# Attention in head pairs: a masked gate bias spread by DMA, K projected transposed, no output transposes

## The chip, the cores and the metric

One core of a Trainium2 chip runs the whole kernel in one launch. The metric is the device time in microseconds (us) of one execution; smaller is better. TensorE (PE) multiplies matrices into PSUM (8 banks of 128 partitions x 512 float32), VectorE (DVE) and ScalarE (ACT) work on PSUM and SBUF, GpSimd (POOL) on SBUF only, and SyncE (SP) issues most DMAs. A matmul keeps one operand stationary (its "weights", up to 128 x 128) and streams the other one past it.

## The reference

A decoder trunk of two layers on 256 tokens of width 1024, float32. Layer 0 mixes tokens with a recurrence (RG-LRU), layer 1 with forgetting attention; each layer has a SwiGLU FFN (hidden width 2816) before and after its mixer, and RMS norms around every part. What the change touches is K, V and the gate, which are computed between the layers, and the attention:

```python
def shared_kv(h, g, w_kv, w_f, b_f):
    hn = rms_norm(h, g)
    kv = (hn @ w_kv).reshape(Bn, S, 2, N_HEADS, HEAD_DIM)      # 16 heads of 64
    k, v = ...
    log_f = jax.nn.log_sigmoid((hn @ w_f + b_f).astype(jnp.float32))
    c = jnp.cumsum(log_f, axis=1).transpose(0, 2, 1)

def forgetting_attention(xq, w_q, w_o, k, v, c):
    q = (xq @ w_q).reshape(...) * (HEAD_DIM ** -0.5)
    for blk in range(S // Q_BLOCK):                            # 2 blocks of 128 queries
        logits = q_block @ k[:, :, :end].T + c[q] - c[k]       # per head
        logits = jnp.where(kpos[None, :] <= qpos[:, None], logits, -jnp.inf)
        p = jax.nn.softmax(logits, axis=-1)
        outs.append(p @ v[:, :, :end])
    return concat(outs) @ w_o
```

## The kernel before

The 256 tokens are two halves t = 0 and 1 of 128. Every weight matrix is read once, in units of 512 KB: `load_raw` issues the DMA on SP's queue into one of 5 raw buffers, and `split` cuts it into an upper part (ACT, L199) and the rest (DVE, L200), each float32r; 9 split units may wait. A product of activations and weights, both cut, takes three matmuls (`mm3`, L207 to L209), or, where the weights are stationary, one of 512 columns (upper and lower activations of both halves side by side) and one of 256 (`mmj`, L222 and L223).

PE's order is the program's order. It is written by hand: `run` and `run_ffn` go through the units with half 1 some units behind half 0, and the units with stationary weights (`tile_items`, `last_items`, through `still`) serve both halves at once on four PSUM banks that are "lent" to them. After each unit, and in the middle of a `still`, `tick` counts down the deferred functions (`defer`) and runs those that are due: transposes, statistics and parameters. The orders of ACT, DVE, POOL and SP are made by a scheduler, which goes by readiness in a model of its own and by the program's order; each engine then runs its queue in order. The memory pools of the FFN and of the attention share addresses: a tile of the next pool waits for the readers of the tile that it covers.

PSUM banks are given out by `bank`: 0 to 3 to accumulators ("mm"), 4 and 5 ("gt"), 6 and 7 ("tr"); `sparebank` takes a "tr" bank, or an "mm" one while 6 is lent.

K is projected like V, with the activations stationary, so that tokens lie on partitions. `heads_T` scales it, appends two columns to each head (a one and the negative gate sum `nck`), and transposes head by head: 8 transposes of 128 x 66 for each half and group of 8 heads. Q goes the same way (with the gate sum `cq` and a one), so that a matmul over 66 rows gives the logits with c[q] - c[k] in them.

The attention of half t goes in groups of four heads (t = 0, 128 keys) or two (t = 1, 256 keys): 4 and 8 groups. `logits` multiplies (L1128), adds the causal mask to the diagonal block (L1129), takes the maximum (L1131) and the exponentials with their sums (L1136). `turn` transposes the exponentials (L1144) and copies them (L1146). `values` multiplies by V with the exponentials stationary (L1155), 64 columns a head, and after 8 heads divides by the sums (L1158, L1160). `output` transposes that (L1168) and cuts it into `oh` and `ol` (L1171, L1172) for the output projection. Step i does logits(i), values(i-3), turn(i-2) and, where 8 heads are done, output. A string gives the order of units and steps ("0" and "1": a unit of half 0 or 1, first of w_q, then of w_o; "a0" and "a1": a step):

```python
    ATT_ORDER = ("0 0 0 0 0 0 0 0 a0 1 a0 1 1 1 a0 1 a0 1 a0 1 a0 a1 1 a0 "
                 "0 a1 a0 a1 0 a1 0 a1 0 a1 0 a1 0 a1 0 a1 0 a1 1 a1 1 a1 1 1 1 1 1 1")
```

Of the kernel before, what the change touches and what calls it, by code (L numbers as in the profile page):

```python
# [16 lines left out]
P = 128  # L17
# [27 lines left out]
def trunk_kernel(ctx: ExitStack, tc: tile.TileContext, A: dict, out: bass.AP):  # L45
# [21 lines left out]
    def bank(kind, hold=False):  # L67

        i = next(i for i in order[kind] if i not in held)
        assert i not in lent, (kind, i)  # L70
# [21 lines left out]
    def sparebank():  # L92
        return bank("mm" if 6 in lent else "tr")
# [125 lines left out]
    def mmj(b, wh, wl, k):  # L219

        tensor_work(3 * S)
        nc.tensor.matmul(pall[:, b, :], wh, xall[:, k, :, :].rearrange("p a b -> p (a b)"), start=k == 0, stop=False)  # L222
        nc.tensor.matmul(pall[:, b, :S], wl, xhi[:, k, :], start=False, stop=k == 7)  # L223
# [135 lines left out]
    state = {"p": 0, "a": 0, "b": 0}  # L359
# [143 lines left out]

    def ffn_items(pool_of, wg, wu, wd, post_g, next_dests, last=False, normed=False, lead=1):
# [4 lines left out]
        def hid_tiles():  # L509
            if not hid:  # L510
                for s in ("hhi", "hlo"):
                    hid[s] = pool_of().tile([P, 2, 22, P], F32R, tag=s, name=nm(s), bufs=1)
# [34 lines left out]
        def total(v, b, m):  # L547

            nc.scalar.activation(v, pall[:, b:b + m, S:], AF.Copy)
            nc.vector.tensor_tensor(v, pall[:, b:b + m, :S], v, ALU.add)  # L550

# [18 lines left out]
        def still(t, u, k0, b0):  # L570
            if k0 == 0:
                assert not set(held) & set(range(b0, b0 + 4)), held.keys()
                lent.update(range(b0, b0 + 4))
            for j in range(2):
                for b in range(4):
                    o = j * 512 + b * P
                    mmj(b0 + b, u.hi[:, o:o + P], u.lo[:, o:o + P], k0 + j)
                if j == 0:
                    tick()
            if k0 == 6:  # L580
                lent.difference_update(range(b0, b0 + 4))

        def tile_items(w, c0, b0, post):
            for k0 in range(0, 8, 2):
                def prep(k0=k0):
                    return split(load_raw(w[k0 * P:(k0 + 2) * P, c0:c0 + 512].rearrange("(k p) n -> p k n", p=P), P, 1024),
                                 P, 1024)

                def work(t, u, k0=k0):
                    still(t, u, k0, b0)  # L590
                    if k0 == 6:
                        post(b0, 4)
                items.append((prep, work))

        def last_items(c0):
            for k0 in range(0, 8, 2):
# [7 lines left out]
                def work(t, u, k0=k0):  # L604
                    still(t, u, k0, 4)
# [27 lines left out]
    def run_ffn(ends, lag_out=LAG):  # L633
# [6 lines left out]
        state["a"] = state["b"] = i2  # L640
        run(n, MID, lag_out)
# [13 lines left out]
    def other_gains():  # L655
# [4 lines left out]
        defer(5, lambda: gains_T(grow, 40, 16))  # L660
# [324 lines left out]
    def dests_l1(t, hid):  # L985
        zx[t] = [hid[s][:, t, :8, :] for s in ("hhi", "hlo")]
        return [(GI["kv"], *zx[t]), main_dest(GI[("ffn1", 1)], t)]
# [3 lines left out]
    def kv_tiles():  # L991
        lp = ctx.enter_context(tc.tile_pool(name="kv", bufs=1, reuse_waits="tile"))
        kv["kT"] = lp.tile([HA, NH, S], F32, name="kT")
        kv["v"] = [lp.tile([P, D], F32, name=f"v{t}") for t in range(2)]
        for n in ("nck", "cq", "lf"):
            kv[n] = [lp.tile([P, NH], F32, name=f"{n}{t}") for t in range(2)]
        kv["bfb"] = lp.tile([P, 2 * NH], F32, name="bfb")[:, :NH]
# [7 lines left out]
        cm = kv["cmask"] = lp.tile([P, P], F32, name="cmask")  # L1005
        nc.gpsimd.memset(cm, 0.0)
        nc.gpsimd.affine_select(out=cm, in_=cm, compare_op=ALU.is_ge, fill=NEG, base=0,
# [355 lines left out]
```

## Time and profile before

| | |
|---|---|
| median of 3 runs | 1009.94 us (1008.15 to 1010.61) |
| the profiled execution | 1007.29 us, its span 1005.6 us |
| granted TensorE clock | 0.999 of full speed |
| PE busy | 991.0 us of the span |
| DVE, ACT, POOL busy | 665.3, 566.1, 51.5 us |
| DMA | 178.90 MB, 178 GB/s on average |

The profile is of one execution. A line such as L1128 is a line of the kernel. PE rows are matmuls, PEld rows their weight loads; a float32 matmul that is not float32r shows as two records, a transpose as one. A matmul's own duration overlaps that of the next one, so its slot is read from the distance of the starts, or from the chain of waits, which is cut at the starts. A groups' row gives: line, engine, operation, output<-input, shapes, count | busy us, mean ns | idle before. A timeline's row gives: start, duration, engine, line and operation, and in brackets the idle time before.

### The profile page before, as it was taken

To read this page: it belongs to the slowest core of one execution; us is meant where nothing else is said; L and a number is where in the kernel's file an instruction comes from. 1 tells how busy PE (TensorE), PEld (TensorE's weight loads), DVE (VectorE), ACT (ScalarE), POOL (GpSimd) and SP (SyncE) were. 2 spreads that over 40 slices of the span, in tenths; PEclk is the share of its full clock that TensorE was granted. 3 is DMA by queue.
4 is the path that set the end of the run, shared out by engine and by line. 5 is a ranking of instruction groups with operands and counts; after the bars stand their busy time and mean duration, and the time that the engine had idled before them with its cause. 6 is when DMAs were issued, how large, how long until landed. Compare 5 with 4: busy or idle time off the path is not lost.

```text
span 1005.6 us, 13910 instructions
## 1 busy us (share of the span) xinstructions
PE 991.0 (99%) x5302; PEld 847.3 (84%) x5302; DVE 665.3 (66%) x768; ACT 566.1 (56%) x742; POOL 51.5 (5%) x113
## 2 busy tenths in 40 slices
PE   8999999999999999999999999999999999999997
PEld 5887888889988888888898888888888888888885
DVE  5877664568998676664695577674477477666642
ACT  5656543559987555543565555553468566555431
POOL 1500000000003000000000000000020020000000
PEclk9999999999999999999999999999999999999999
DMA  6877656565427666545476766655555057665431
GB/s 230 280 263 204 190 161 197 154 181 151 141 78 250 212 188 187 188 158 185 114 227 218 209 191 184 192 189 168 168 168 168 2 188 237 184 199 195 155 121 42
DMA packets 91864, 178.90 MB, mean 178 GB/s; under 512 B 11790, under 2 KB 31318, under 8 KB 91798
## 3 DMA queue, kind: packets, MB, share of 16 engines
q1 hardware_dynamic: 90550, 176.89, 56.8%
q10 hardware_dynamic: 608, 1.06, 0.3%
q8 instruction: 41, 0.67, 0.3%
q0 software_dynamic: 640, 0.07, 0.1%
q14 instruction: 25, 0.20, 0.1%
HBM read 176.95 MB, written 1.05 MB: 177 GB/s over the span
## 4 chain that ended last, share of the span: by engine, by line
PE 70%; issue 21%; ACT 4%; DVE 4%; POOL 1%; DMA 0%; DVEq 0%; POOLq 0%; ACTq 0%
PE pall L222 21%; PE pall L223 11%; PE pall L209 10%; PE pall L208 10%; PE pall L207 10%; PE pall L845 1%; DVE wlo L200 1%; PE pall L214 1%; PE pall L215 1%; PE pall L216 1%; PE pall L1128 1%; ACT junk L236 1%; PE pall L1155 1%; ACT whi L199 1%; PE pall L1026 1%
## 5 line engine op out<-in xcount | busy, mean ns | idle before, releaser
L200 DVE TENSOR_TENSOR wlo<-raw,whi 128x1024 fp32r<-128x1024 f32 (+4 forms) x329 | 394.6, 1206 | 242.3 <-ACT whi L199 241.8
L199 ACT ACTIVATE whi<-raw 128x1024 fp32r<-128x1024 f32 (+4 forms) x329 | 342.1, 1044 | 290.3 <-PE pall L209 125.6
L222 PE MATMUL pall<-xall,whi 128*128 128x512 f32 x1216 | 424.7, 395 | 0.0
L223 PE MATMUL pall<-xall,wlo 128*128 128x256 f32 x1216 | 338.4, 278 | 0.0
L222 PEld LDWEIGHTS pall<-xall,whi 128*128 128x128 f32 x1216 | 228.1, 188 | 53.3
L223 PEld LDWEIGHTS pall<-xall,wlo 128*128 128x128 f32 x1216 | 228.8, 188 | 0.2
L207 PE MATMUL pall<-whi,hhi 128*128 128x512 f32 (+2 forms) x432 | 166.0, 384 | 0.0
L209 PE MATMUL pall<-whi,hlo 128*128 128x512 f32 (+2 forms) x432 | 165.0, 382 | 0.0
L208 PE MATMUL pall<-wlo,hhi 128*128 128x512 f32 (+2 forms) x432 | 164.8, 382 | 0.0
L209 PEld LDWEIGHTS pall<-whi,hlo 128*128 128x128 f32 x432 | 81.1, 188 | 15.1
L208 PEld LDWEIGHTS pall<-wlo,hhi 128*128 128x128 f32 x432 | 81.2, 188 | 14.7
L207 PEld LDWEIGHTS pall<-whi,hhi 128*128 128x128 f32 x432 | 81.2, 188 | 14.6
L207 PE MATMUL pall<-whi,xall 128*128 128x512 f32 (+2 forms) x168 | 67.1, 400 | 0.1
L208 PE MATMUL pall<-wlo,xall 128*128 128x512 f32 (+2 forms) x168 | 64.9, 386 | 0.4 <-DVE wlo L1226 0.2
L209 PE MATMUL pall<-whi,xall 128*128 128x512 f32 (+2 forms) x168 | 64.9, 386 | 0.1
L229 POOL TENSOR_SCALAR nv<-ss 128x1 f32<-128x1 f32 x24 | 10.9, 453 | 749.8 <-ACT junk L236 749.6
L208 PEld LDWEIGHTS pall<-wlo,xall 128*128 128x128 f32 x168 | 31.7, 189 | 7.5 <-DVE wlo L200 1.2
L209 PEld LDWEIGHTS pall<-whi,xall 128*128 128x128 f32 x168 | 31.5, 188 | 7.1 <-DVE xall L259 1.1
L207 PEld LDWEIGHTS pall<-whi,xall 128*128 128x128 f32 x168 | 31.6, 188 | 5.7 <-ACT xall L254 0.5
L567 ACT ACTIVATE hhi<-prod 128x1024 fp32r<-128x1024 f32 (+1 forms) x21 | 20.6, 980 | 25.2 <-DVE prod L563 25.2
L300 DVE SCALAR_TENSOR_TENSOR t<-pall,rstd,gb 128x512 f32<-128x512 f32 x16 | 11.9, 748 | 26.7 <-ACT junk L236 26.7
L557 ACT ACTIVATE sil<-sil 128x1024 f32<-128x1024 f32 (+1 forms) x21 | 20.6, 982 | 15.1 <-DVE sil L556 15.0
(190 smaller groups left out, 974.2 us busy)
## 6 DMA issues: line engine op xcount, KB each, us to landing
raw<-in_ffn_w_down_dram SPq DMA_DIRECT2D x88, 512.0 KB
raw<-in_ffn_w_up_dram SPq DMA_DIRECT2D x80, 512.0 KB
raw<-in_ffn_w_gate_dram SPq DMA_DIRECT2D x79, 512.0 KB
raw<-in_rg_w_in_dram SPq DMA_DIRECT2D x20, 504.0 KB
raw<-in_rg_w_out_dram SPq DMA_DIRECT2D x10, 504.0 KB
raw<-in_ffn_w_gate_dram SPq DMA_DIRECT2D x18, 256.0 KB
raw<-in_ffn_w_up_dram SPq DMA_DIRECT2D x16, 256.0 KB
raw<-in_w_kv_dram SPq DMA_DIRECT2D x8, 512.0 KB
```

Source lines behind the costliest of these rows:

```text
L199: nc.scalar.activation(hi[:parts, c:c + m], rawv[:, c:c + m], AF.Copy)
L200: nc.vector.tensor_tensor(lo[:parts, c:c + m], rawv[:, c:c + m], hi[:parts, c:c + m].bitcast(F32), ALU.subtract)
L207: nc.tensor.matmul(ps, xh, wh, start=first, stop=False)
L208: nc.tensor.matmul(ps, xh, wl, start=False, stop=False)
L209: nc.tensor.matmul(ps, xl, wh, start=False, stop=last)
L214: nc.tensor.matmul(ps, wh, xh, start=first, stop=False)
L222: nc.tensor.matmul(pall[:, b, :], wh, xall[:, k, :, :].rearrange("p a b -> p (a b)"), start=k == 0, stop=False)
L223: nc.tensor.matmul(pall[:, b, :S], wl, xhi[:, k, :], start=False, stop=k == 7)
L229: nc.gpsimd.tensor_scalar(v, ss[:, 0:1], ss[:, 1:2] if n == 2 else 0.0, D * EPS * f * f, ALU.add, ALU.add)
L300: nc.vector.scalar_tensor_tensor(t1[n], pf[n], r_in, gb[:, n * 512:(n + 1) * 512], ALU.mult, ALU.mult)
L557: nc.scalar.activation(s, s, AF.Silu)
L567: nc.scalar.activation(hv, pv, AF.Copy)
```

## The change

- **K** is projected with its weights stationary (`tile_items` with the moving operand of the normed stream, `z_moving`), so that it comes out with head dimensions on partitions, two heads on 128. It is scaled by the row of factors `rcp` and not transposed. For this the two FFN tiles `hhi` and `hlo` become one.
- **Q** is transposed in pairs of heads, 4 transposes instead of 8 for each half and group of 8 heads, without extra columns.
- **The gate** is no longer in the matmul. The gate sums are turned (`rows`), written to DRAM as 16 x 256, read back onto all 128 partitions (`nb0` 128 keys, `nb1` 256 keys for each head; 1 and 2 MB) on SP's queue, masked by POOL, and added to the logits in one DVE addition per step. c[q] is left out, since it drops out of the softmax.
- **Logits** take the two heads of a pair from partitions 0-63 and 64-127, into two banks; the sums are divided out before `turn`.
- **Values** have V stationary (64 columns) and the transposed exponentials moving, and write the two heads of a pair to partitions 0-63 and 64-127 of the result, which thus comes out transposed; `output` is gone.
- A step is values(i-3), turn(i-2), logits(i), and the order string begins the steps one unit earlier.
- `defer` has a flag `calm`: such a function runs only outside the first and the last unit of a `still` block. It is set for `rg_params`, the gains, `running` and `rows`. `sparebank` takes an "mm" bank whenever one of 0 to 3 is neither held nor lent.

```diff
     def sparebank():
-        return bank("mm" if 6 in lent else "tr")
+        return bank("mm" if any(i not in held and i not in lent for i in range(4)) else "tr")
...
-    def defer(n, fn):
-        pend.append([n, fn])
+    def defer(n, fn, calm=False):
+        pend.append([n, fn, calm])
...
-            if p[0] < 0:
+            if p[0] < 0 and not (p[2] and state["edge"]):
...
-    def mmj(b, wh, wl, k):
+    def x_moving(k):
+        return xall[:, k, :, :], xhi[:, k, :]
+
+    def mmj(b, wh, wl, k, moving):
         tensor_work(3 * S)
-        nc.tensor.matmul(pall[:, b, :], wh, xall[:, k, :, :].rearrange("p a b -> p (a b)"), start=k == 0, stop=False)
-        nc.tensor.matmul(pall[:, b, :S], wl, xhi[:, k, :], start=False, stop=k == 7)
+        both, upper = moving(k)
...
+        nc.tensor.matmul(o, wh, both, start=k == 0, stop=False)
+        nc.tensor.matmul(oh, wl, upper, start=False, stop=k == 7)
...
+    def still(u, k0, b0, moving=x_moving):
...
+        state["edge"] = k0 in (0, 6)
...
-        defer(5, lambda: gains_T(grow, 40, 16))
+        defer(5, lambda: gains_T(grow, 40, 16), True)
...
+        kv["ckT"] = lp.tile([NH, S], F32, name="ckT")
+        kv["dram"] = ctx.enter_context(tc.tile_pool(name="scratch", bufs=1, space=bass.MemoryType.DRAM)).tile(
+            [NH, S], F32, name="ckd")
...
+    def heads_T(pool, ps, t, n, scale, dst):
+
+        tok = pool.tile([P, 512], F32, tag="htok", name=nm("htok"), bufs=2)
+        nc.vector.tensor_scalar(tok, ps, rs[t][:, 0:1], scale, ALU.mult, ALU.mult)
+
+        def turn():
+            tp = bank("mm")
             for j in range(4):
...
+                nc.tensor.transpose(tp[:, j * P:(j + 1) * P], tok[:, j * P:(j + 1) * P], ident)
+            nc.scalar.activation(dst[:, 4 * n:4 * n + 4, :].rearrange("p a b -> p (a b)"), tp, AF.Copy)
+        defer(2, turn)
 
     def post_k(n):
-        return lambda t, ps: heads_T(pools["f"], ps, t, n, 1.0, (None, kv["nck"][t]), kv["kT"][:, :, t * P:(t + 1) * P])
+        def f(b, m):
+            kk = pools["f"].tile([P, 16 * HA], F32, tag="prod", name=nm("kk"), bufs=1)[:, :1024]
+            v = kk.rearrange("p (a b) -> p a b", a=4)
+            total(v, b, m)
+            nc.vector.tensor_tensor(kv["kT"][:, 4 * n:4 * n + 4, :], v, rcp["v"].unsqueeze(1).to_broadcast([P, 4, S]), ALU.mult)
+        return f
...
+    def rows(t):
+        pc = sparebank()
+        nc.tensor.transpose(pc[:NH, :P], kv["nck"][t], ident)
+        nc.vector.tensor_copy(kv["ckT"][:, t * P:(t + 1) * P], pc[:NH, :P])
+        if t == 1:
+            nc.sync.dma_start(kv["dram"], kv["ckT"])
...
-        proj_items(A["w_kv"], n * 512, 512, z_x, post_k(n))
+        tile_items(A["w_kv"], n * 512, 4 - 4 * n, post_k(n), z_moving)
...
     def att_tiles():
         ap = pools["a"]
...
+        src = kv["dram"].rearrange("h k -> (h k)").partition_broadcast(P).rearrange("p (h k) -> p h k", h=NH)
...
+            nb = ap.tile([P, NH, (t + 1) * P], F32, name=f"nb{t}")
+            nc.sync.dma_start(nb, src[:, :, :(t + 1) * P])
+            v = nb[:, :, t * P:]
+            nc.gpsimd.affine_select(out=v, in_=v, compare_op=ALU.is_ge, fill=NEG, base=0,
+                                    pattern=[[0, NH], [-1, P]], channel_multiplier=1)
...
         def logits(hg):
...
+            c = 4 + (hg % 2) * 2
+            lg = pall[:, c:c + 2, :S]
+            for j in range(np_):
+                for b in range(2):
+                    p = hg * np_ + j
+                    nc.tensor.matmul(lg[:, b, j * w:(j + 1) * w], att["q"][t][b * HD:(b + 1) * HD, p, :],
+                                     kv["kT"][b * HD:(b + 1) * HD, p, :w], start=True, stop=True)
...
+            nc.vector.tensor_tensor(v, v, bias, ALU.add)
...
+            nc.vector.reciprocal(sm, sm)
+            nc.vector.tensor_tensor(pe, pe, sm.unsqueeze(2).to_broadcast([P, per, w]), ALU.mult)
 
         def turn(hg):
-            tp = trbank()
+            tp = bank("mm", again=True)
...
         def values(hg):
...
+                        nc.tensor.matmul(po[b * HD:(b + 1) * HD, o:o + P], kv["v"][k][:, hd * HD:(hd + 1) * HD],
+                                         pT[:, (b * np_ + j) * nk + k, :], start=k == 0, stop=k == nk - 1)
+            if (p0 + np_) % 4 == 0:
...
+                nc.scalar.activation(oh_v, po, AF.Copy)
+                nc.vector.tensor_tensor(ol_v, po, oh_v.bitcast(F32), ALU.subtract)
...
-    ATT_ORDER = ("0 0 0 0 0 0 0 0 a0 1 a0 1 1 1 a0 1 a0 1 a0 1 a0 a1 1 a0 "
-                 "0 a1 a0 a1 0 a1 0 a1 0 a1 0 a1 0 a1 0 a1 0 a1 1 a1 1 a1 1 1 1 1 1 1")
+    ATT_ORDER = ("0 0 0 0 0 0 0 a0 0 a0 1 1 1 a0 1 1 a0 1 1 a0 1 a1 0 a0 0 a1 0 a0 0 a1 0 a1 0 a1 0 a1 0 a1 1 a1 1 a1 1 a1 1 a1 1 1 1 1")
...
-    defer(40, rg_params)
+    defer(40, rg_params, True)
...
-    run(n_kv)
+    run_ffn((n_v, n_kv, n_kv))
```

More of the change, by code (lines that the diff above doesn't have):

```diff
@@ L65, in trunk_kernel, with bank @@
     held = {}
-    def bank(kind, hold=False):
-        i = next(i for i in order[kind] if i not in held)
-        assert i not in lent, (kind, i)
+    def bank(kind, hold=False, again=False):
+        free = [i for i in order[kind] if i not in held and i not in lent]
+        i = free[-1 if again else 0]
         order[kind].remove(i)
@@ L604, in work @@
                 def work(t, u, k0=k0):
[L605 removed]
+                    still(u, k0, 4)
                     if k0 == 6:
```

182 lines of the change are left out of this document (82 added, 100 removed).

## The prediction, made before the changed kernel was run

> **What bounds the kernel now.** I read the page first: the busy times (part 1) and the shares of the chain (part 4).
>
> ```profile
> PE 991.0 (99%) x5302; PEld 847.3 (84%) x5302; DVE 665.3 (66%) x768; ACT 566.1 (56%) x742; POOL 51.5 (5%) x113
> PE 70%; issue 21%; ACT 4%; DVE 4%; POOL 1%; DMA 0%; DVEq 0%; POOLq 0%; ACTq 0%
> ```
>
> TensorE (PE) is never free; VectorE (DVE) and ScalarE (ACT) have a third and more of the span to spare. So the time is the length of PE's instruction stream plus its few waits, and what counts is how much stream an edit takes away, and whether a new wait opens. Next I asked for PE's waits: ten lines, from 2.1 us down to 0.2, about 7 us in all. The largest stands below them in PE's timeline:
>
> ```profile
> PE pall L699 <- issue: 2.1, 1, 2.1
> PE pall L208 <- DVE wlo L200: 0.2, 1, 0.2
> ```
>
> ```profile
> 82.58 0.28 PE L223 MATMUL pall<-xall,wlo 128*128 128x256 f32 x1
> 85.00 0.27 PE L699 MATMUL pall<-ident,prow 88*126 88x88 f32 x1 [2.13 <-issue]
> 85.05 0.48 PE L222 MATMUL pall<-xall,whi 128*128 128x512 f32 x1
> ```
>
> Last I read the chain of waits from 730 to 810 us, where the attention lies. It runs almost only over PE there, so its durations are slots in PE's stream: the transposes of Q and K (L1026), of the exponentials (L1144) and of the output (L1168), the logits (L1128) and the values (L1155). One block of each (a group of four heads has eight records, of two heads with 256 keys four):
>
> ```profile
> 745.20 0.44 PE pall L1026 x4
> 749.30 0.89 PE pall L1128 x8
> 778.77 0.87 PE pall L1128 x4
> 779.64 0.84 PE pall L1155 x8
> 780.48 0.45 PE pall L1144 x4
> ```
>
> **The change, term by term.** *Transposes.* The groups by line give their numbers:
>
> ```profile
> L1026 PE MATMUL pall<-ident,htok 128*66 128x128 f32 x64 | 9.6, 272 | 0.0
> L1168 PE MATMUL pall<-ident,ot 128*128 128x128 f32 x16 | 2.5, 280 | 0.1
> ```
>
> 64 head transposes are 16 blocks of four: 8 for K, 8 for Q. K's all go (it is now projected transposed), Q's are halved (a pair of heads fills 128 rows), and the 4 output blocks go (values now writes its result transposed). 16 blocks x 0.44 = **-7.0 us**; nothing covers PE, so all of it counts.
>
> *The wait at L699.* `rg_params` is deferred by 40 ticks and lands where its bank is still being emptied. `calm` puts it off to the middle of a unit. I take the 2.13 us idle as gone, **-2.1**; what is late next is a weight unit, and at 85 us the following matmul comes 0.05 us behind, so those weights are there.
>
> *K projection.* 96 matmuls of 512 columns become 64 pairs of 512 and 256: 49,152 columns either way. Rows of both kinds in PE's timeline:
>
> ```profile
> 539.43 0.40 PE L207 MATMUL pall<-whi,hhi 128*128 128x512 f32 x1
> 542.85 0.39 PE L207 MATMUL pall<-whi,hhi 128*128 128x512 f32 x1
> 560.11 0.39 PE L222 MATMUL pall<-xall,whi 128*128 128x512 f32 x1
> 563.58 0.39 PE L222 MATMUL pall<-xall,whi 128*128 128x512 f32 x1
> ```
>
> 15 matmuls in 3.42 us are 0.228 each, 10 pairs in 3.47 us 0.347 each: 96 x 0.228 = 21.9 against 64 x 0.347 = 22.2, **+0.3**. The moving operand is now read in pieces of 128 columns, which no row shows; a separate 256-column matmul costs half of a 512-column one (0.347 less 0.23 is 0.12), so shorter pieces have no visible price, and I take none. K's evacuation, one ACT copy and two DVE operations per half, lies beside the next 32 pairs, 11 us on the other four banks.
>
> *The gate's rows.* Two small transposes come in (`rows`). The nearest row is a small transpose between full matmuls, where a pair's L223 rows are otherwise 0.347 apart:
>
> ```profile
> 46.15 0.28 PE L223 MATMUL pall<-xall,wlo 128*128 128x256 f32 x1
> 46.36 0.25 PE L157 MATMUL pall<-ident,grow 40*128 40x40 f32 x1
> 46.54 0.49 PE L222 MATMUL pall<-xall,whi 128*128 128x512 f32 x1
> 46.87 0.28 PE L223 MATMUL pall<-xall,wlo 128*128 128x256 f32 x1
> ```
>
> 0.72 - 0.347 = 0.37 us for this one, against 0.11 for one of a block of four: 0.2 to 0.8 for two, I take **+0.5**.
>
> *Logits and values in half arrays.* Record counts stay, as the float32 matmul still takes two records. Today they cost 4 x 0.89 + 8 x 0.87 + 12 x 0.84 = 20.6 us. Now two heads sit in the two row halves (logits) or column halves (values). No row shows two matmuls in two halves. One bound: they run one after the other as today, 0. Other bound: the second record of one head overlaps the first of the other, so a block of eight takes five slots and one of four takes three. That saves 3 x 0.11 in each of 4 logit and 12 value blocks and 0.22 in each of 8 logit blocks: 1.3 + 4.0 + 1.7 = -7.0. Against it stands entering and leaving such a block: L157, with 40 rows, is the only row of a part of the array in a full stream, and it costs 0.37 - 0.11 = 0.26 more than a full-size transpose. 24 blocks x 0.26 = +6.2; the lower end is 0. So -7.0 to +6.2; I take the middle, **0**, since both rows and bounds are of equal size.
>
> The Trainium skill (TensorEngine Tiling (Array Packing), Key Properties) says that changing the tiling mode drains TensorE, which speaks against this edit; the L157 row agrees with it, and by that rule alone the sum would be 6.2 higher. The same page (Theoretical Speedup) gives up to 2x for a dimension of 64; as an estimate from it, 20.6 us would fall to 10.3, and no trace here shows it.
>
> *Waits in the softmax.* A step is now values, turn, logits, instead of logits, values, turn. Its chain today:
>
> ```profile
> 786.14 1.03 PE L1128 MATMUL pall<-kT,qT 66*128 66x256 f32 x4
> 787.21 0.43 DVE L1129 TENSOR_TENSOR pall<-pall,cmask 128x256 f32<-128x256 f32 x1 [2.39 <-PE pall L1128]
> 789.84 0.21 ACT L1136 ACTIVATION_READ_ACCUMULATOR pe<-pall,mx 128x1 f32 x1
> 794.94 0.61 PE L1144 MATMUL pall<-ident,pe 128*128 128x128 f32 x4
> 791.59 0.69 DVE L1160 TENSOR_TENSOR ot<-pall,sm 128x512 f32<-128x512 f32 x1 [0.41 <-PE pall L1155]
> 797.18 0.20 DVE L1158 RECIPROCAL sm<-sm 128x8 f32<-128x8 f32 x1 [1.72 <-ACT pe L1136]
> 797.03 0.60 ACT L1171 ACTIVATE oh<-pall 128x512 fp32r<-128x512 f32 x1
> ```
>
> From the logits' start at 786.14 to the exponentials' end at 790.05 it takes 3.9 us, and their transpose comes at 794.94: 4.9 us to spare. The new chain adds 0.26 (the addition covers 512 columns), a reciprocal (0.20) and a product (0.69, like L1160) ahead of the transpose: 5.1 with nothing in between, some 5.4 with two hand-overs. The new gap from logits to their transpose is their own 0.87, a unit (six matmuls of 0.228, 1.37), values 0.84, turn 0.45, logits 0.87, a unit, and values 0.84: 6.6 us. So about 1 us is spare. What can stand in between is a weight split:
>
> ```profile
> L200 DVE TENSOR_TENSOR wlo<-raw,whi 128x1024 fp32r<-128x1024 f32 (+4 forms) x329 | 394.6, 1206 | 242.3 <-ACT whi L199 241.8
> L199 ACT ACTIVATE whi<-raw 128x1024 fp32r<-128x1024 f32 (+4 forms) x329 | 342.1, 1044 | 290.3 <-PE pall L209 125.6
> ```
>
> One of them, 1.21 or 1.04 us, eats what is spare. Where two steps meet without a unit, and at the last output unit, which follows values(7) at once and needs the copy `oh` (0.60) and a subtraction like L1160 (0.69), PE waits 1 to 1.5 us each time. I take **+3.0** in all, from 0 to 8.
>
> *The bias.* 1 MB and 2 MB are broadcast from DRAM through SP's queue, and GpSimd masks each; DVE adds. What SP, GpSimd, ACT's table load and the DMA engines take today:
>
> ```profile
> 735.75 0.39 PE L209 MATMUL pall<-whi,hlo 128*128 128x512 f32 x1
> 731.38 6.13 SPq L187 DMA_DIRECT2D raw<-in_attn_w_o_dram  x4
> 738.51 0.33 SPq L352 DMA_DIRECT2D gb<-in_mix_post_g_dram  x1
> 741.02 18.88 SPq L187 DMA_DIRECT2D raw<-in_attn_w_o_dram  x4
> 317.05 0.29 POOL L1007 TENSOR_SCALAR_AFFINE_SELECT cmask<-cmask 128x128 f32<-128x128 f32 x1
> 752.69 1.28 ACT L1136 ACT_TABLE_LOAD   x1
> 750.00:800.00 50.00, 49.62 (x313) 43.12 (x312) 29.17 (x45) 33.84 (x95) 0.24 (x2) 1.00 0.28 85
> GB/s 230 280 263 204 190 161 197 154 181 151 141 78 250 212 188 187 188 158 185 114 227 218 209 191 184 192 189 168 168 168 168 2 188 237 184 199 195 155 121 42
> ```
>
> The first copy must wait for the FFN's tiles in the same memory, last read at 736 us (the first row). SP has a hole at 738 to 741. At some 200 GB/s, which weight loads reach in many of the 40 slices of the last row, 1 MB takes 5 us: landed by 744. The mask covers 16 times L1007's columns, at most 16 x 0.29 = 4.6 us: ready by 749. The first logits come at 736 + 7 units + transposes, about 747, and PE first waits for their result at the third step, four units and two steps later, about 755; the chain (5.4, and 1.28 for a table load) fits within a microsecond. The second copy has until about 767. DMA is at 28% there, so the loads behind it have room. Cost **0**, if the order on SP's queue is that. DVE gets about 8 us more work (12 products less 4, and the longer additions) in a stretch where it is busy 29 of 50 us: covered, but for the chain above.
>
> **Sum.** -7.0 - 2.1 + 0.3 + 0.5 + 0 + 3.0 + 0 = -5.3 us. The profiled execution took 1007.29 us with a span of 1005.6, and would take 1002.0 with 1000.3. Its time lies 2.65 below the median of the runs, so the median goes from 1009.94 to **1004.6**.
>
> **Rivals.** *Half arrays pair without a price*: -7.0 instead of 0, so 997.6. For it: PE has no other work between; against it: L157's 0.26. Chance 0.17. The Trainium skill's factor of two, cited above, stands on this side.
>
> *The softmax sets the step.* If one or two splits lie in each chain, 5.4 + 2 x 1.21 = 7.8 against 6.6, PE waits 1.2 us at most of the 12 turns, and with the ends some 8 to 11 us instead of 3: 1009.6 to 1012.6. Against it: in the second half's later steps no splits run. Chance 0.18. Half arrays at L157's price without pairing (+6.2), with 3 of waits, end at the same place, 1010.8; I count them here.
>
> *The bias comes late.* If SP holds the first copy behind the four loads that stand at 741.02 and wait until 759.9 for buffers, it lands near 765 and is masked by 769. PE reaches the first transpose at 755 and needs the bias some 6 us before that, so it waits about 769 + 6.7 - 755 = 21 us: 1001.6 + 21 = 1022.6 with the other waits covered by this one. It decides from 748 us on: each microsecond later than that is one of PE's. For it: SP's queue is in order and its loads wait long; against: the hole at 738. Chance 0.12: slower.
>
> *The calm tasks and the bank choice change nothing* (the L699 wait only moves): 2.1 less gain, 1006.7. Chance 0.05, and the forecast keeps 0.48.
>
> **Numbers.** About 0.3% (3 us) is what a measurement of this kernel can tell from no change: below 1006.9 is faster, above 1013.0 slower. The forecast's own range is 999 to 1010. Faster: most of the forecast (0.42), all of the first rival (0.17), the last one (0.04) and a bit of the second (0.03): 0.66. Slower: the bias (0.12), a tail of the second (0.04) and of the forecast (0.02): 0.18. The rest is 0.16. The range, 995 to 1013, takes in both bounds of the half arrays and the second rival, and leaves out the late bias.
>
> **What the profile after would show.** Right: no transposes of K or of the output, 16 of Q; L699's successor without the 2 us; blocks of logits and values whose slots differ from 0.89, 0.87 and 0.84 by little either way; a few PE waits on ACT or DVE between 736 and 806, 3 us in all. Wrong: value blocks of 0.5 us (half arrays pair), PE waits at most turns (softmax), a PE wait of over 5 us at the first turn with a DMA behind it (bias), or K pairs well over 0.347.

## The result

The changed kernel takes **1005.41 us** (median of 8 runs, 1004.71 to 1007.71) against 1008.22 for the kernel before in the same comparison: ratio 0.9968 (95% interval 0.9956 to 0.9980), **2.8 us faster**, where 5.3 were forecast. A second comparison gave 1005.72 against 1007.91, ratio 0.9973 (0.9962 to 0.9984). The profiled execution took 1004.95 us with a span of 1003.2, 2.34 and 2.4 less than before. The page after answers the two lines read first:

```profile
PE 985.8 (98%) x5272; PEld 831.9 (83%) x5272; DVE 676.1 (67%) x784; ACT 562.1 (56%) x732; POOL 50.8 (5%) x97
PE 68%; issue 22%; ACT 5%; DVE 4%; POOL 1%; DMA 0%; DVEq 0%; POOLq 0%; ACTq 0%
```

PE is still the bound and 5.2 us less busy, but its span fell by 2.4 only: it waits more. Its waits (engine, line, what it waited for: us in total, times, longest), the two largest of those that the kernel before doesn't have:

```profile
PE pall L209 <- DVE ol L1207: 2.8, 3, 1.7
PE pall L207 <- ACT oh L1206: 1.0, 1, 1.0
```

Both lie in the attention. Where the difference arose is read from the starts of the same work in the two traces:

| PE begins | before | after | difference | within the stage |
|---|---|---|---|---|
| down projection, first FFN | 139.23 | 137.85 | -1.38 | -1.4 |
| down projection, second FFN | 441.03 | 440.02 | -1.01 | +0.4 |
| down projection, third FFN (V and K lie before it) | 675.20 | 671.71 | -3.49 | -2.5 |
| last `rstd_rows`, behind the attention | 825.40 | 821.38 | -4.02 | -0.5 |
| down projection, fourth FFN | 938.92 | 936.74 | -2.18 | **+1.8** |

The fourth FFN, which the change doesn't touch, gives back 1.8 us of 4.0. Both stand there on the same instructions; in PE's timeline 231 pairs before, and 227 after, lie between these starts:

```profile
850.18 0.39 PE L222 MATMUL pall<-xall,whi 128*128 128x512 f32 x1
930.25 0.40 PE L222 MATMUL pall<-xall,whi 128*128 128x512 f32 x1
```

```profile
850.17 0.40 PE L232 MATMUL pall<-xall,whi 128*128 128x512 f32 x1
930.38 0.40 PE L232 MATMUL pall<-xall,whi 128*128 128x512 f32 x1
```

That is 0.3466 and 0.3533 us a pair at a granted clock of 1.00 in both: 288 pairs x 6.7 ns = 1.9 us. The first FFN after holds both rhythms (24 pairs between the first two of these rows, and 24 between the last two), and they change at `rg_params`:

```profile
60.98 0.40 PE L232 MATMUL pall<-xall,whi 128*128 128x512 f32 x1
69.46 0.40 PE L232 MATMUL pall<-xall,whi 128*128 128x512 f32 x1
86.42 0.24 PE L712 MATMUL pall<-ident,prow 88*126 88x88 f32 x1
94.86 0.39 PE L232 MATMUL pall<-xall,whi 128*128 128x512 f32 x1
103.18 0.39 PE L232 MATMUL pall<-xall,whi 128*128 128x512 f32 x1
```

8.48 / 24 = 0.3533 before L712, 8.32 / 24 = 0.3467 after it. In the attention itself the blocks are shorter, as the chain of waits shows (values, turn, and logits with 256 keys):

```profile
777.29 0.59 PE pall L1200 x8
777.88 0.59 PE pall L1186 x4
778.47 0.63 PE pall L1162 x4
```

Values 0.59 for 0.84, logits 0.63 for 0.87 (0.65 for 0.89 in the first half), but the turn 0.59 for 0.45.

### The profile page after: what moved, and what is told of

Same layout as the page of the kernel before. It is cut to its first block, busy times and chain, and to the rows that moved or that the text cites. A ratio compares the mean times of both kernels' runs of the same rounds, so it can differ in the third digit from the quotient of the medians.

```text
span 1003.2 us, 13846 instructions
## 1 busy us (share of the span) xinstructions
PE 985.8 (98%) x5272; PEld 831.9 (83%) x5272; DVE 676.1 (67%) x784; ACT 562.1 (56%) x732; POOL 50.8 (5%) x97
## 3 DMA queue, kind: packets, MB, share of 16 engines
q10 hardware_dynamic: 608, 1.06, 0.3%
HBM read 180.09 MB, written 1.06 MB: 181 GB/s over the span
## 4 chain that ended last, share of the span: by engine, by line
PE 68%; issue 22%; ACT 5%; DVE 4%; POOL 1%; DMA 0%; DVEq 0%; POOLq 0%; ACTq 0%
PE pall L232 23%; PE pall L233 12%; PE pall L207 9%; PE pall L209 9%; PE pall L208 9%; PE pall L858 1%; PE pall L214 1%; PE pall L215 1%; PE pall L216 1%; ACT junk L246 1%; DVE wlo L200 1%; ACT whi L199 1%; POOL rstd L241 1%; PE pall L255 1%; DVE h L316 1%
## 5 line engine op out<-in xcount | busy, mean ns | idle before, releaser
L207 PE MATMUL pall<-whi,hid 128*128 128x512 f32 (+2 forms) x400 | 153.1, 383 | 0.5 <-ACT v L1109 0.5
L209 PE MATMUL pall<-whi,hid 128*128 128x512 f32 (+2 forms) x400 | 152.4, 381 | 0.0
L208 PE MATMUL pall<-wlo,hid 128*128 128x512 f32 (+2 forms) x400 | 152.3, 381 | 0.0
L207 PEld LDWEIGHTS pall<-whi,hid 128*128 128x128 f32 x400 | 75.1, 188 | 14.6 <-ACT v L1109 0.8
L208 PEld LDWEIGHTS pall<-wlo,hid 128*128 128x128 f32 x400 | 75.1, 188 | 13.6
L209 PEld LDWEIGHTS pall<-whi,hid 128*128 128x128 f32 x400 | 75.1, 188 | 13.7
L604 ACT ACTIVATE hid<-prod 128x1024 fp32r<-128x1024 f32 (+1 forms) x21 | 20.6, 981 | 23.0 <-DVE prod L600 23.0
L594 ACT ACTIVATE sil<-sil 128x1024 f32<-128x1024 f32 (+1 forms) x21 | 20.6, 982 | 14.3 <-DVE sil L593 14.2
```

Source lines behind the costliest of these rows:

```text
L207: nc.tensor.matmul(ps, xh, wh, start=first, stop=False)
L208: nc.tensor.matmul(ps, xh, wl, start=False, stop=False)
L209: nc.tensor.matmul(ps, xl, wh, start=False, stop=last)
L594: nc.scalar.activation(s, s, AF.Silu)
L604: nc.scalar.activation(hv, pv, AF.Copy)
```

## The experiments

In the changed kernel the transposes of `rg_params` are L712, logits L1162, turn L1186, values L1200, the copy and the subtraction of the values (`oh`, `ol`) L1206 and L1207, the mask L1135. Each run was compared with the kernel before on its chip.

| run | median us | ratio to before (95%) |
|---|---|---|
| after_again | 1005.72 | 0.9973 (0.9962 to 0.9984) |
| nopair | 1011.65 | 1.0040 (1.0026 to 1.0053) |
| calm_alone | 1006.42 | 0.9977 (0.9966 to 0.9988) |
| k_rows | 1009.68 | 1.0015 (1.0005 to 1.0024) |
| nudge | 1005.58 | 0.9978 (0.9967 to 0.9988) |
| order1 | 1004.66 | 0.9967 (0.9955 to 0.9978) |
| order2 | 1001.17 | 0.9931 (0.9920 to 0.9943) |
| order3 | 1003.62 | 0.9953 (0.9937 to 0.9970) |
| order3_tvl | 1001.73 | 0.9933 (0.9917 to 0.9950) |
| order2_tvl | 1001.81 | 0.9935 (0.9921 to 0.9949) |
| order4_tvl | 1005.16 | 0.9968 (0.9955 to 0.9981) |
| best | **999.19** | 0.9906 (0.9887 to 0.9924) |

**Do the halves overlap? (nopair)**

```
-            for j in range(np_):
-                for b in range(2):
-                    p = hg * np_ + j
+            b, p0 = hg % 2, per * (hg // 2)
+            for i in range(per):
...
-                                     kv["kT"][b * HD:(b + 1) * HD, p, :w], start=True, stop=True)
+                                     kv["kT"][b * HD:(b + 1) * HD, p0 + i, :w], start=True, stop=True)
...
```

> The changed kernel with its heads grouped so that neighbouring matmuls of a group sit in the same half of the array (all four, or both, heads of a group even or all odd); the records, the half-array mode and its entries and exits stay. Theory A (neighbours in two halves overlap, and that is why a logits block takes 0.65 and 0.63 and a values block 0.59 us): the blocks go back to about 0.85-0.89, 24 blocks times 0.24 = about 5.5 us slower than the changed kernel, some 3 us slower than the kernel before. Theory B (the blocks are short because an operand of 64 rows or columns is quicker by itself): blocks stay at 0.6 and the time within 1 us of the changed kernel. In both, the pair rhythm of the stages before 736 us is that of the changed kernel, 0.3530 in the first FFN up to 86 us, 0.3535 in the second, 0.3467 in the third.

Its step in PE's timeline (values L1198, turn L1185, logits L1161):

```profile
781.54 1.09 PE L1198 MATMUL pall<-pT,v 128*64 128x128 f32 x8
782.56 0.66 PE L1185 MATMUL pall<-ident,pe 128*128 128x128 f32 x4
783.14 1.13 PE L1161 MATMUL pall<-kT,qT 64*128 64x256 f32 x4
784.20 0.50 PE L207 MATMUL pall<-whi,oh 128*128 128x512 f32 x1
```

Theory A holds, and the price is larger than expected: values 1.02, logits 1.06, so 0.43 per block, and the attention takes 103.7 us instead of 95.2 (from the third FFN's transposes to the last `rstd_rows`) though PE waits 1.5 us less. The 1.02 and 1.06 even stand above the 0.84 and 0.87 of the kernel before; the rows of the next section show that this is the price of going into and out of the half array, not of the records in it. The turn stays at 0.58, so its longer slot comes with the half array and not with the overlap.

**What a passage costs (order3_tvl; order3 is its base, below)**

A passage is here a change between the whole array, its column halves and its row halves.

```
-            if 0 <= i - 3 < G:
-                s.append(lambda i=i: values(i - 3))
             if 0 <= i - 2 < G:
                 s.append(lambda i=i: turn(i - 2))
+            if 0 <= i - 3 < G:
+                s.append(lambda i=i: values(i - 3))
             if i < G:
                 s.append(lambda i=i: logits(i))
```

> order3 with the order in a step turn, values, logits instead of values, turn, logits. Theory A (each change between whole and half array costs PE about 0.1 to 0.17 us): a step has three changes less one, 11 steps, about 0.8 to 1.5 us less in slots. Rival (a change from column halves to row halves costs as much as one to the whole array): slots add up to the same within 0.2 us. In both, turns come 0.6 us earlier behind their exponentials, so waits at turns may add up to 1 us each where they are short of time now.

Its step with all three blocks in PE's timeline (turn L1187, values L1201, logits L1163), up to the next turn:

```profile
777.25 0.60 PE L1187 MATMUL pall<-ident,pe 128*128 128x128 f32 x4
777.78 0.66 PE L1201 MATMUL pall<-pT,v 128*64 128x128 f32 x8
778.37 0.70 PE L1163 MATMUL pall<-kT,qT 64*128 64x256 f32 x4
779.00 0.50 PE L207 MATMUL pall<-whi,oh 128*128 128x512 f32 x1
780.50 0.60 PE L1187 MATMUL pall<-ident,pe 128*128 128x128 f32 x4
```

A step with its unit lasts 3.25 us; in the changed kernel it is 3.40 (777.22 to 780.62), in nopair 4.25 (781.54 to 785.79). Before it is 3.55, from the row of 786.14 in the prediction to this one of the same timeline:

```profile
789.69 1.03 PE L1128 MATMUL pall<-kT,qT 66*128 66x256 f32 x4
```

So the new order of a step saves 0.15 us. That values to logits, from column to row halves, costs nothing doesn't follow, since the slots of 0.59 and 0.63 hold a passage in every order. The price is seen in windows so narrow that only the last records of one block and the first of the next lie in them: values to turn and turn to logits in the changed kernel, values to logits in order3_tvl, values to turn in nopair.

```profile
777.60 0.28 PE L1200 MATMUL pall<-pT,v 128*64 128x128 f32 x2
777.81 0.33 PE L1186 MATMUL pall<-ident,pe 128*128 128x128 f32 x1
778.20 0.27 PE L1186 MATMUL pall<-ident,pe 128*128 128x128 f32 x1
778.40 0.48 PE L1162 MATMUL pall<-kT,qT 64*128 64x256 f32 x1
778.16 0.28 PE L1201 MATMUL pall<-pT,v 128*64 128x128 f32 x2
778.37 0.49 PE L1163 MATMUL pall<-kT,qT 64*128 64x256 f32 x2
782.25 0.38 PE L1198 MATMUL pall<-pT,v 128*64 128x128 f32 x2
782.56 0.33 PE L1185 MATMUL pall<-ident,pe 128*128 128x128 f32 x1
```

Where one record lasts 0.27, two last 0.28 in the first and the fifth row, so they begin within 0.01 us: the halves overlap completely. In nopair two last 0.38, so they begin 0.11 apart, as in the kernel before (0.45 for a turn of four). From the last record to the next block it is 0.20 or 0.21 us, for values to logits too, where 0.11 is the step inside a block. So the passage from column to row halves costs as much as the others: the rival's mechanism. A step still gets shorter because it has three passages instead of four (its unit is followed by a turn, both in the whole array). Over the whole attention 7 of 47 passages go, and without the waits and the dip of the clock in order3, told of below, it is 0.6 us shorter than there, between theory A's 0.8 to 1.5 and the rival's 0.2.

**Where the waits come from (order1, order2, order3)**

The longest wait of the changed kernel, by the timeline's rows of DVE and, last, of PE:

```profile
788.61 0.69 DVE L312 TENSOR_TENSOR t<-pall,gb 128x512 f32<-128x512 f32 x1
789.54 1.42 DVE L316 SCALAR_TENSOR_TENSOR h<-t,rstd,h 128x512 f32<-128x512 f32 x2 [0.25 <-POOL rstd L241]
790.88 0.68 DVE L1207 TENSOR_TENSOR ol<-pall,oh 128x512 fp32r<-128x512 f32 x1
791.61 0.50 PE L209 MATMUL pall<-whi,ol 128*128 128x512 f32 x1 [1.69 <-DVE ol L1207]
```

The subtraction that the second half's first output unit needs stands on DVE behind the end of the first half (`enter`, L312 and L316). order1 begins the second half's steps one unit earlier, order2 two:

```
-  ... a0 1 1 a0 1 a1 0 a0 0 a1 0 a0 0 a1 0 a1 0 a1 0 a1 0 a1 1 a1 1 a1 1 a1 1 a1 1 1 1 1
+  ... a0 1 a0 1 a1 a0 1 a1 0 a0 0 a1 0 a1 0 a1 0 a1 0 a1 0 0 a1 1 a1 1 a1 1 a1 1 1 1 1 1   (order1)
+  ... a0 1 a0 1 a1 a0 1 a1 a0 0 a1 0 a1 0 a1 0 a1 0 a1 0 a1 0 0 a1 1 a1 1 a1 1 1 1 1 1 1   (order2)
```

> The changed kernel with the steps of the second half begun one unit earlier, so that an output unit no longer follows directly on the step that finishes its input. Theory A (the waits of 1.69, 1.04, 0.68, 0.41 and 0.30 us stand because the copy and the subtraction of the values come too late for the output unit behind them): those at the output units go, about 3 us faster than the changed kernel, with new waits at turns below 1 us. Rival (ACT and DVE are short of time over the whole stretch, so a wait only moves): PE waits about 4 to 5 us again, at turns or at the accumulators, and the time stays within 1 us of the changed kernel.

> As order1, with the second half's steps two units earlier. Theory A: waits of PE between 736 and 806 us below 1.5 us in all, 3 to 4 us faster than the changed kernel. Rival: the first output unit of the second half now follows the last of the first half closely and waits 1 to 2 us for its banks, and turns wait; no better than order1 or the changed kernel.

order1 bears out the rival: the attention is 0.3 us shorter, and PE still waits 4.6 us in it, mostly at turns, 1.3 of them at `ol`. order2 bears out theory A at the output units, which wait no longer, and not at the turns; its attention is 2.3 us shorter than the changed kernel's. The largest of PE's waits that are left in it:

```profile
PE pall L1186 <- ACT qT L1032: 1.7, 3, 0.8
PE pall L1186 <- DVE pe L1180: 1.0, 1, 1.0
```

Its other 1.9 us is rhythm: its fourth FFN runs at 0.3467. order3 then moves one logits block ahead of a unit and gives the turn another bank than the head transposes (`again=not state.pop("qbank", False)`, and the last head transpose one tick earlier).

> As order2, with the second half's first logits ahead of a unit, and the bank of a head transpose no longer the next turn's. Theory A: the waits of 0.32, 0.61 and 0.82 us behind the head transposes and the 0.96 at the second half's first turn go: attention 2 to 2.7 us shorter than in order2, 4 to 5 shorter than in the changed kernel. Rival (ACT's and DVE's weight splits set when the exponentials come): the waits move to the neighbouring turns, within 0.7 us of order2. The fourth FFN's rhythm adds 0 or 1.9 us to either.

The three waits behind the head transposes went, others came (2.0 at one turn, 1.0 and 1.0 elsewhere): the rival. Its attention is 2.2 us longer than order2's, and 1.7 of them are no wait at all but a dip of the clock (0.91 over 20 us), told of below.

**The rhythm (nudge, after_again, calm_alone, best)**

```
   still():  if j == 0: tick()
+            if k0 == 2 and state["n"] in NUDGE:
+                nc.tensor.transpose(sparebank()[:126, :88], ident[:88, :126], ident[:88, :88])
```

> The changed kernel with eleven unread small transposes (88 x 126) put between pairs: three in the first, second and fourth FFN, two in the third. Theory A (the pair stream runs at one of two rhythms, 0.3467 or 0.3533 us, which an interruption can change and which then holds to the next one): stretches between the transposes differ within a stage, some of the slow ones of the changed kernel (first FFN up to 86 us, all of the second and of the fourth) become fast, and each stretch of about 100 pairs that changes is worth 0.7 us; a transpose itself costs 0.03 to 0.37. Between 2 us faster and 2 us slower in all, and the sum of the stretches accounts for it within 0.5 us. Theory B (the rhythm is set by what the stage reads: its tiles' places, its DMA traffic): the stretches keep the changed kernel's rhythm, stage by stage, and the time is 0.5 to 3 us longer, by the transposes alone.

The second FFN there, 24 pairs between the first two and between the last two rows:

```profile
361.56 0.39 PE L232 MATMUL pall<-xall,whi 128*128 128x512 f32 x1
369.88 0.39 PE L232 MATMUL pall<-xall,whi 128*128 128x512 f32 x1
386.52 0.24 PE L534 MATMUL pall<-ident 88*126 88x88 f32 x1
395.10 0.40 PE L232 MATMUL pall<-xall,whi 128*128 128x512 f32 x1
403.58 0.40 PE L232 MATMUL pall<-xall,whi 128*128 128x512 f32 x1
```

0.3467 ahead of the transpose, 0.3533 behind it, while the stage goes on reading the same tiles. Theory A holds in that an interruption sets the rhythm, and theory B falls. In that stage the rhythm was slow, fast (from 353), slow (387), fast (421), in the fourth FFN slow, fast, slow, fast. The first, the second and the fourth FFN each got some 0.6 us shorter; the stage of the third lost 1.2, since its second transpose made some 150 fast pairs slow. The profile's span is 0.7 us shorter, and the median stayed where it was.

> The changed kernel once more, with its own profile and times on the same chip as the others. If the rhythm of a stretch of pairs is drawn anew in each execution, some of the four stages differ from the first profile (first FFN slow up to 86 us and fast behind it, second slow, third fast, fourth slow), and the time moves by 0.9 to 1.9 us for each; if the program fixes it, all four are as before and the time is 1004.5 to 1005.5. The sum without the rhythm (all stages fast in both kernels) would be about 5 us below the kernel before.

All four stages had the rhythm of the first profile, so it isn't drawn anew each time. The time of this execution, 1007.02, is another matter (below).

```
-    defer(40, rg_params)
+    defer(40, rg_params, True)      # with defer's flag and the edge state, in the kernel before
```

> The kernel before with one edit: rg_params is put off until a unit in the middle of a tile, as the change does. The prediction's term: the wait of 2.13 us goes and the time falls by 2.1 us. Rival (the rhythm of the pairs changes with the interruption): the wait goes, but the stretch before or behind it runs at 0.3533 instead of 0.3467 us a pair, some 130 or 150 pairs, which gives back 0.9 to 1.0 us; 0.1 to 1.2 us faster.

Here L702 is `rg_params`:

```profile
85.13 0.28 PE L223 MATMUL pall<-xall,wlo 128*128 128x256 f32 x1
85.25 0.24 PE L702 MATMUL pall<-ident,prow 88*126 88x88 f32 x1
85.28 0.48 PE L222 MATMUL pall<-xall,whi 128*128 128x512 f32 x1
```

The wait is gone. Behind the transpose 148 pairs run at 0.3533, where the kernel before has 0.3467 on both sides of its waiting L699: 1.0 us back, and 1.6 us remain by the trace (1.5 by the medians). That lies between the rival's range (up to 1.2) and the term (2.1); the mechanism is the rival's, and 0.2 us of the rest stand ahead of the first FFN's pairs, which begin at 35.85 instead of 36.08. In twelve profiles in which these transposes stand alone between pairs, the rhythm differs on their two sides, either slow and then fast or the reverse.

> order3_tvl with two of the unread small transposes of the nudge run: one 12 pairs or so into the pairs of the second FFN and one as early in the fourth, the two stages that ran slow throughout in order3_tvl (0.3533). Theory A (an interruption resets the rhythm; in the nudge run and at rg_params each of five such transposes in a slow stretch left it fast): both stages run at 0.3467 from there on, about 260 pairs each x 6.7 ns = 1.7 us each, less 0.1 for a transpose: 3.2 us faster than order3_tvl, 998.5. Rival (the rhythm behind an interruption is chance): one or both stay slow, 998.5 to 1002, and the times of the runs spread over that.

```
+    NUDGE = (11, 33)      # and the lines of nudge, in order3_tvl
```

999.19 us, the fastest version here: 0.9938 of the changed kernel's 1005.41, by the two medians. But theory A was wrong in one word: the second FFN went from slow to fast and lost 1.5 us, while the fourth this time came in fast (0.3467) and the transpose made it slow (0.3533). A single transpose of this kind doesn't reset the rhythm, it mostly **changes** it: of the eleven that stand alone between pairs in nudge and best, nine did. Why the fourth FFN starts fast in some kernels and slow in others wasn't settled. A version without the second transpose was not run.

**K alone (k_rows)**

```
-  tile_items(A["w_kv"], n * 512, 4 - 4 * n, post_k(n), z_moving)
+  proj_items(A["w_kv"], n * 512, 512, z_x, ... heads_T(..., kv["kT"][:, :, t * P:(t + 1) * P]))
```

> The changed kernel with K projected in rows again, as before the change: 96 matmuls of 512 columns and four blocks of four transposes (a pair of heads each) instead of 64 pairs. The prediction's terms give 4 x 0.44 = 1.8 for the blocks and -0.3 for the projection: 1.4 to 1.5 us longer between 500 and 553 us than the changed kernel. Rival (reading the moving operand in pieces of 128 columns had a price that the blocks' going hid): less than 1 us longer, or shorter. The whole time also carries the fourth FFN's rhythm, 0 or -1.9 us.

From the second FFN's to the third's down projection it took 3.9 us longer than the changed kernel, against 1.5 expected; 1.8 us of it are two waits of PE on this version's own scaling of K on DVE, which shares one tile. So it can't say what the pieces of 128 columns cost. The changed kernel's trace can; 19 of K's pairs lie between these starts:

```profile
526.93 0.40 PE L232 MATMUL pall<-hid,whi 128*128 128x512 f32 x1
533.52 0.39 PE L232 MATMUL pall<-hid,whi 128*128 128x512 f32 x1
```

6.59 / 19 = 0.347, the fast rhythm: the pieces have no price.

**A long wait and the clock (order2_tvl, order4_tvl, and after_again)**

> order2 with turn, values, logits in a step and the banks of order3. Theory A (a change between whole and half array costs PE 0.1 to 0.17 us, and between column and row halves nothing): 0.15 us less for each of the 8 steps that hold all three, 1.2 us less in slots than order2; waits 1 to 3 us as there. With the fourth FFN at the fast rhythm 999.5 to 1000.5, at the slow one 1001.4 to 1002.4.

```
   order4_tvl:  ... a0 1 1 a0 a1 1 a0 a1 0 a0 0 a1 0 a1 0 a1 0 a1 0 a1 0 0 a1 1 a1 1 a1 1 a1 1 1 1 1 1
```

> As order2_tvl, with one more unit ahead of the first half's third turn and of the second half's first turn. Theory A (the three waits of 0.90, 0.76 and 0.53 us at these turns come from exponentials that are late by just that): they go, and a wait of up to 1 us comes in where the fifth output unit of the second half follows the last values by one unit; 0.5 to 1.5 us faster than order2_tvl at the same rhythm. Rival (the splits' order on ACT and DVE makes the exponentials late wherever the turns are): the waits stay, and the time is that of order2_tvl within 0.5 us.

order2_tvl came out within its range for the slow rhythm, which its fourth FFN had. order4_tvl fits neither theory: two of the three waits went, 1.2 stayed at the third turn, and 1.5 and 1.3 came in later, at a turn and at `ol`; its attention is 2.0 us longer than order2_tvl's. Part of what these orders lost is seen only in the clock. Windows of 4 us in after_again (busy times of PE, PEld, DVE, ACT and POOL, then the granted clock, the DMA share and GB/s):

```profile
788.00:792.00 4.00, 2.49 (x19) 1.38 (x18) 3.49 (x7) 2.25 (x7) 0.98 (x2) 1.00 0.00 0
792.00:796.00 4.00, 3.82 (x16) 2.38 (x16) 2.31 (x4) 2.76 (x7) 1.03 (x3) 0.57 0.01 2
```

and the wait of its first window in PE's timeline:

```profile
792.18 0.53 PE L209 MATMUL pall<-whi,ol 128*128 128x512 f32 x1 [1.69 <-DVE ol L1207]
```

Right behind the wait of 1.69 us the clock is at 0.57 for 4 us (finer windows show 0.50 from 792.52 to 795.93, 3.4 us), and 1.7 us are lost. The first profile of the same kernel has the same wait and no such dip: its attention is 1.5 us shorter. Over all fourteen profiles five of the nine with a wait of 1.19 us or more from 24 us on have a dip behind it, and none of the five whose waits stay below 1 us; k_rows has one more at 8.07 us, behind waits of 0.61 and 0.96.

What tells them apart shows when the dips are counted back from the end of the profile, where PE is done and the clock falls to 0.50 in every profile. Each dip begins a whole multiple of 3.413 us before that: 62 in after_again (from 792.52 to 1004.15), 69 in order3, 66 in order2_tvl, 68 in order4_tvl, 61 and 292 in k_rows. So the dips begin at borders of windows of 3.413 us that run through the execution wherever the work stands. PE's idle time in the window that ends where a dip begins:

| | after_again | order3 | order2_tvl | order4_tvl | k_rows | k_rows |
|---|---|---|---|---|---|---|
| dip begins | 792.52 | 763.87 | 773.59 | 767.04 | 796.55 | 8.07 |
| idle in the window before | 1.69 | 1.99 | 1.62 | 1.73 | 1.70 | 1.58 |

In the first profile of the changed kernel a border at 791.30 cuts the wait of 1.69 into 1.38 and 0.31, in nudge one at 790.38 does so, and neither dips. Of all other windows up to PE's last instruction none holds more than 1.45 us of idle time, but for one: the wait at L699 in the kernel before leaves 1.83 us in a window (81.28 to 84.69), and no dip follows. So idle time alone doesn't decide, and what else does stays open.

The twelve times of after_again fall into two groups, 1004.5 to 1005.0 and 1006.5 to 1007.0; five of order2, without such a wait, lie within 0.6 us. That the upper group is the dip is likely and was seen in one profile of each group only.

## Why the prediction was right or wrong

| term | forecast | measured |
|---|---|---|
| wait at L699 | -2.1 | -1.0 up to the second FFN's end |
| K: blocks, projection, gate rows | -2.7 | -2.5 |
| Q and output blocks, half arrays, softmax waits | -3.5 + 0 + 3.0 = -0.5 | -0.5, the waits in it +4.4, so -1.4 for the half arrays if the blocks gave their -3.5 |
| bias | 0 | 0 |
| rhythm of the fourth FFN | not in the sum | +1.8 |
| sum | -5.3 | -2.2 in the traces, -2.8 by the medians |

**K** came as worked out, down to the pairs' 0.347. The gate's rows cost less than 0.5: a small transpose slips in between pairs (0.02 us from its start to the next matmul's), and the pair behind it lasts 0.44 instead of 0.347, 0.1 us for each:

```profile
542.64 0.27 PE L1074 MATMUL pall<-ident,nck 128*16 128x128 f32 x1
542.66 0.47 PE L232 MATMUL pall<-hid,whi 128*128 128x512 f32 x1
543.10 0.40 PE L232 MATMUL pall<-hid,whi 128*128 128x512 f32 x1
```

**The wait at L699** went as said, 2.13 us; the step that failed is "what is late next is a weight unit". Next was the rhythm: 132 pairs ahead of L712 at 0.3533 give back 0.9. Another 0.4 went between the first and the second FFN, 0.3 of it at one wait on `hn` (0.60 us for 0.32).

**Half arrays at 0** came within 1.4 us by luck: both bounds were too small, and the gain and the price nearly cancel. The text let only the second record of one head overlap the first of the next, so that a block of eight takes five slots and one of four takes three. The records begin two at a time, so it is four and two, half of the 20.6 us: 10.3 saved instead of at most 7.0. That leaves 10.3 - 1.4 = 8.9 us for the passages (bound: 6.2). Each of the 24 blocks is entered and left, and one values block follows straight on a logits block, so there are 47 passages of about 0.19 us; this price is an estimate from the remainder, and the rows above show 0.09 to 0.10 of it ahead of the new block's first record. The first rival was right on the mechanism and wrong on "without a price"; its sign, value blocks of 0.5, came as 0.59, which is 0.44 and a share of two passages. The Trainium skill (TensorEngine Tiling (Array Packing), Theoretical Speedup) gives up to 2x for a dimension of 64. Inside a block the trace agrees; with its passages a values block is 1.4x as fast as before (0.59 for 0.84). The same page's Key Properties say that changing the tiling mode drains TensorE. The trace agrees at each of the three kinds of passage whose rows are shown (0.20 to 0.21 for 0.11), column halves to row halves among them.

**Waits** were 4.4 instead of 3.0, within the 0 to 8, but at another place. The chain from the logits to their turn, which the text worked through, holds: PE waits 0.3 us at one turn in all. The others but one (0.30 on the result of DVE's L312) stand at output units that come soon behind the `values` they read. The prediction had this wait for the last output unit (1 to 1.5 us; measured 1.04 + 0.68) and overlooked the earlier places (1.69, and 0.30 + 0.41). The longest is not the hand-over's own length: ACT had copied `oh` by 788.84 (it began at 788.23 and took 0.61), but DVE came to the subtraction at 790.88 only, behind `enter`. Where two steps meet without a unit (781.80 and 782.62 in PE's timeline), PE doesn't wait, nor at the steps in general: the rival "softmax sets the step" didn't come.

**The bias** went out as forecast ahead of SP's waiting weight loads and was not late; the timeline's rows of SP's queue, POOL's first mask and the first addition on DVE:

```profile
732.98 4.72 SPq L1133 DMA_DIRECT2D nb<-ckd  x2
741.47 2.06 POOL L1135 TENSOR_SCALAR_AFFINE_SELECT nb<-nb 128x2048 f32<-128x2048 f32 x1 [1.82 <-DMA nb<-ckd]
744.76 0.70 DVE L1169 TENSOR_TENSOR pall<-pall,nb 128x512 f32<-128x512 f32 x1 [3.10 <-PE pall L1162]
```

A mask takes 2.0 us instead of at most 4.6; the addition waits for the logits, not for the bias.

**The sum** was mis-sized by the term that it didn't hold. It took 0.347 as the pair's fixed price, read in the third FFN alone; read in the second, the kernel before would have shown 0.3533 beside it. That term, 0.9 + 1.8, is the distance from -5.3 to -2.2 within half a microsecond. That the forecast time of 1004.6 lies within 0.8 us of the measured 1005.41 is luck as well: it started from 1009.94, the median of three runs, and over eight runs the kernel before took 1008.22, so a base that was 1.7 too high covered most of a gain that was 2.5 too large.

## What to carry to other kernels

In these runs two matmuls in two halves of the array overlapped completely where neighbours alternated, and not at all where they didn't; every passage between whole array, column halves and row halves cost about 0.19 us. So count the passages, and order the blocks so that there are few: a step of turn, values, logits has one less. When an edit gives a consumer its operand by a longer hand-over (copy, then subtraction), look for every unit that follows the producer at once, not for the last alone, and for what stands ahead of the hand-over on its engine. And before a 1 us effect is explained by an edit, compare the stages that the edit doesn't touch, instruction by instruction.

## What the hardware showed that was not expected

The stream of 512- and 256-column matmuls runs in one of two rhythms, 0.3467 or 0.3533 us a pair at full clock, holds it over hundreds of pairs, and mostly changes it at a single 88 x 126 transpose; what the two states are stays open.

A PE wait far shorter than 3.4 us can be followed by 3.4 us at half clock (1.7 us lost): six dips begin at borders of windows of 3.413 us, each behind a window with 1.58 to 1.99 us of idle time. The Trainium skill (TensorE: Matmul & The Clock Gate, The HAM clock gate) tells of half clock after an idle window of some 3.4 us that runs freely. The traces agree on the window's length and on its running freely, which is why one wait of 1.69 us is followed by a dip in one execution and not in another; but a window that was about half idle was enough here, and one with 1.83 us of idle time was not.
